# A fixed order for the first half units of a two-layer decoder kernel, filler products in its pause, and a rearranged last tile

## Chip, cores and metric

The kernel runs on one core of a Trainium2 chip. The metric is the device time of one execution in microseconds, as the median of several runs.

## What is computed

The reference is a decoder trunk of two layers on 256 tokens of width 2048, in float32. Layer 0 mixes with RetNet retention (8 heads), layer 1 with MoBA attention (16 heads, one block of 256, so plain causal attention with a bias); each is followed by a gated MLP with a causal convolution of width 3. In short:

```python
for i in range(2):
    hn = rms_norm(h, mix_norm[i])
    h = h + (retention_mixer if i == 0 else moba_mixer)(hn, ...)
    h = h + conv_ffn(rms_norm(h, ffn_norm[i]), ...)
return rms_norm(h, final_norm)        # rms_norm: x * rsqrt(mean(x*x) + 1e-6) * gain
```

The retention mixer begins with `h @ ret_w_in`, whose first columns are q and k of head 0; q and k are rotated by a table of cosines and sines (rope). All weights are float32, about 0.48 GB in all, and each is read once.

## The kernel before, in words

**Products in three parts.** A float32 product is made from rounded high parts and the rest: every operand is split into hi and lo, and hi·hi, hi·lo and lo·hi are summed. ScalarE (ACT) makes the high part `wh` by a copy that rounds (L214); VectorE (DVE) makes the low part `wl = raw - wh` (L215). Both are done by `split_to`.

**Units and half units.** Weights come in units of 1 MB (`raw`, four buffers), issued on SyncE's (SP's) queue in `issue_dma` and `first_dmas`. Each unit is used in halves of 128 x 1024 (a few in four parts). `halves` is the list of all of them in order; `run` (L244) walks through it: for half i it first emits the splits up to i + ahead (`issue_split`), then the products of half i, then what `after` has put off to this point. `ahead` is 0 for i = 0, 2 up to i = 7, and 3 from there. `wh` and `wl` have four buffers each.

**The first eight halves** are q and k of head 0, taken in turn (`emit_pairs`): halves 0, 2, 4, 6 belong to q, halves 1, 3, 5, 7 to k; unit 0 gives halves 0 and 2, unit 1 halves 1 and 3, unit 2 halves 4 and 6, unit 3 halves 5 and 7. Each half has four blocks c, and a block four products (`panel_b`): two with `wh` against 512 columns of `hT` (hi and lo of x beside each other, L329) and two with `wl` against 256 (L332). From half 8 on come the v and g products of head 0 (`panel_s`, L374), which use a scheme with seven products in place of eight for some blocks and need extra sums on DVE.

**hT.** x is transposed by TensorE (PE) in `to_T` (L500, `x_T` calls it) with an identity matrix; ACT multiplies the result by the gain into the high part (L503), DVE makes the low part (L506). The first two chunks of 128 come at the very start (`x_T(0, 2)`), the next two in the middle of half 0 (`rest`, hung into `midway[0]`), four each in the middle of halves 1, 3 and 5.

**The scale.** ACT squares x and sums (`square_t`, L517, `square(j)` for four column blocks j, two instructions each). `make_rB` sums these (L532), adds eps (L525), raises to -1/2 on POOL (L526), and spreads the result over columns: for each of two row tiles DVE makes a diagonal matrix (L541, one buffer for both) and PE multiplies it with ones (L542). `use_rope` multiplies the rope table by it (L685), and `ret_qk` (L700 to L706) turns finished q or k with the table. `ret_begin` puts the squares off to steps 1, 2, 4, 6 and `make_rB` to step 6.

**Order on an engine.** The instructions are traced in the program's order, and a scheduler then lays them out for each engine: earlier traced ones come first among those that it takes to be ready. So a square or a low part may move far ahead of its place in the program, if its inputs are there. Nothing in this kernel fixes an order beyond the data.

**Warm-up.** PE multiplies ones by ones eight times at the start (L630; each float32 product of this kind is two instructions).

**The end.** The last panel gives its results bank by bank; `last_bank` (L894) adds the residual (L904), squares on ACT (L906, the last 512 columns in two pieces of 256), multiplies by the final gain (L911), and after the last piece sums the squares (L914), raises to -1/2 on POOL (L916), scales four column blocks j on ACT (L922, j = 1, and j = 2 for t = 0) or DVE (L924), and stores each (L925) from ACT's queue where ACT scaled, otherwise from SP's.

Of the kernel before, what the change touches and what calls it, by code (L numbers as in the profile page):

```python
# [17 lines left out]
P = 128  # L18
D = 2048
S = 256  # L20
# [6 lines left out]
LOOKAHEAD = 3  # L27
WARMUP = 8


def constants():
# [17 lines left out]
    return {  # L49
        "c_ident": np.eye(P, dtype=np.float32),  # L50
        "c_rope": np.ascontiguousarray(rope),
# [5 lines left out]
def layouts(a):  # L57

    def cols(v):
        return v.reshape(-1, P).T  # L60

    gains = np.concatenate([cols(a["mix_norm"]), cols(a["ffn_norm"]), cols(a["ret_gn"])], 1)
    taps = np.concatenate([a["ffn_conv_w"], a["ffn_conv_b"][:, None]], 1).reshape(2, 4, 2 * NFB, P)
    return {"l_gains": np.ascontiguousarray(gains), "l_taps": np.ascontiguousarray(taps.transpose(3, 0, 1, 2))}
# [31 lines left out]
def build(tc, a, out):  # L96
# [15 lines left out]

    ident = cst.tile([P, P], F32, name="ident")
    h = cst.tile([P, 2, D], F32, name="h")
# [3 lines left out]
    cst.tile([P, 16], F32, name="gap1")  # L118
    gains = cst.tile([P, 96], F32, name="gains")
    cw = [cst.tile([P, 4, 2 * NFB], F32, name=f"cw{i}") for i in range(2)]  # L120
# [62 lines left out]
    def issue_split(i):  # L183
# [8 lines left out]
        if i == 0:  # L192
# [11 lines left out]

            x_T(0, 2)
            split(slice(0, 512))
            midway[0] = rest
        else:
# [4 lines left out]
    def split_to(hi, lo, src):  # L213
        act.activation(hi, src, AF.Copy)  # L214
        dve.tensor_tensor(lo, src, hi.bitcast(F32), op=ALU.subtract)  # L215

# [24 lines left out]
    def after(n, fn):  # L241
        later.append([state["mm"] + n, fn])

    def run():  # L244
        n = len(halves)
        while state["mm"] < n:
            i = state["mm"]
            ahead = 0 if i == 0 else 2 if i < 8 else LOOKAHEAD
            while state["split"] <= min(i + ahead, n - 1):
                issue_split(state["split"])  # L250
                state["split"] += 1
            halves[i]()
            state["mm"] += 1
            while True:
                due = [t for t in later if t[0] <= state["mm"]]
                if not due:
                    break
                later.remove(due[0])
                due[0][1]()
        for t in sorted(later, key=lambda t: t[0]):  # L260
            t[1]()
# [52 lines left out]
    def panel_b(w, n0, xT, done, before=None):  # L314

        box, items = {}, []
        for k0 in range(0, KC, 4):
            def mm(wh, wl, k0=k0):
# [5 lines left out]
                for c in range(4):  # L324
                    k = k0 + c
                    if c == 2 and state["mm"] in midway:
                        midway[state["mm"]]()
                    for b in range(2):
# [160 lines left out]
    def mm3(dst, lh, ll, rh, rl, start, stop):  # L489
        pe.matmul(dst, lhsT=lh, rhs=rh, start=start, stop=False)  # L490
        pe.matmul(dst, lhsT=lh, rhs=rl, start=False, stop=False)  # L491
        pe.matmul(dst, lhsT=ll, rhs=rh, start=False, stop=stop)  # L492

    def to_T(dstT, k0, src, g0, n):

        for c0 in range(0, n, 2):
            pt = aux_tile().rearrange("p (i s) -> p i s", s=S)
            for i in range(2):
                for t in range(2):
                    pe.transpose(pt[:, i, t * P : (t + 1) * P], src(t, c0 + i), ident)  # L500
            for i in range(2):
                g = gains[:, g0 + c0 + i : g0 + c0 + i + 1]
                act.activation(dstT[:, k0 + c0 + i, :S], pt[:, i, :], AF.Copy, scale=g)  # L503
            for i in range(2):
                g = gains[:, g0 + c0 + i : g0 + c0 + i + 1]
                dve.scalar_tensor_tensor(dstT[:, k0 + c0 + i, S:], pt[:, i, :], g,  # L506
                                         dstT[:, k0 + c0 + i, :S].bitcast(F32), op0=ALU.mult, op1=ALU.subtract)
# [4 lines left out]
    def x_T(c0, n):  # L512
        to_T(hT, c0, lambda t, c: h[:, t, (c0 + c) * P : (c0 + c + 1) * P], c0, n)

    def square_t(j, t):
        junk = scr.tile([P, 512], BF16, name="junk")
        act.activation(junk, h[:, t, j * 512 : (j + 1) * 512], AF.Square, accum_out=ssq[:, t, j : j + 1])  # L517

# [100 lines left out]
    dma0 = nc.scalar.dma_start  # L619
    dma0(ident, a["c_ident"])  # L620
    dma0(gains, a["l_gains"])
    dve.memset(ones, 1.0)
# [5 lines left out]
    warmup = aux_tile()  # L628
    for _ in range(WARMUP):
        pe.matmul(warmup[:, :P], lhsT=ones, rhs=ones, start=True, stop=True)  # L630

# [168 lines left out]
    def ret_begin():  # L800
        for i in (1, 2, 3):
            midway[2 * i - 1] = lambda i=i: x_T(4 * i, 4)
        for j in range(4):
            after(1 + j if j < 2 else 2 * j, lambda j=j: square(j))
        after(6, lambda: make_rB(use_rope))
# [88 lines left out]
    def last_bank(t, n, acc):  # L894
# [22 lines left out]
        for j in range(4):  # L917
# [197 lines left out]
```

## Time and profile before

| | us |
|---|---|
| median of 3 runs (2568.09 to 2571.22) | 2570.52 |
| the profiled execution, its own time | 2570.77 |
| its span, first to last instruction | 2569.0 |
| PE busy in the span | 2555.9 (99%) |
| DVE busy | 2072.8 (81%) |
| ACT busy | 1432.1 (56%) |
| mean share of the granted TensorE clock | 0.998 |

Engine names are PE, PEld (weight load, beside PE), DVE, ACT, POOL, SP. A busy share is a mean over stages; the start, the long middle and the end have different limits, and the change touches the first and the last. "Idle before" in a row is the time in which the engine stood still ahead of a group, with the instruction that ended it. Instructions of one kind that follow each other are merged in a timeline; a few matmul records can be missing.

### The profile page before, as it was taken

Reading aid. Unit: us, or ns where it says so; the run is one execution under the profiler, and the core shown is the slowest. Engines: PE = TensorE matmul, PEld = TensorE weight load, DVE = VectorE, ACT = ScalarE, POOL = GpSimd, SP = SyncE. Lnnn points to the kernel's source line nnn. Section 1 sums busy time; section 2 is a strip of 40 time slices with the busy share of each in tenths; the row PEclk is TensorE's granted clock in tenths of the full one; section 3 lists DMA queues with packets and bytes.
Section 4 is the critical chain, followed back from the end, with each engine's and each line's share of the span. In section 5 each row is a group of like instructions: output and inputs, shape, how many; then the busy total and the mean of one; then the engine's idle time right before and its main releaser. Section 6 shows DMA issues by size and latency. Waiting matters only on the chain.

```text
span 2569.0 us, 34327 instructions
## 1 busy us (share of the span) xinstructions
PE 2555.9 (99%) x13288; PEld 2179.2 (85%) x13288; DVE 2072.8 (81%) x2708; ACT 1432.1 (56%) x1848; POOL 10.2 (0%) x24
## 2 busy tenths in 40 slices
PE   9999999999999999999999999999999999999998
PEld 7888888888888888888888888888888888888887
DVE  7888888898877777777988866668877777779897
ACT  6555555555555555555555555455655555555554
POOL 0000000000000000000000000000000000000000
PEclk9999999999999999999999999999999999999999
DMA  7665655555555555555565655555655555556664
GB/s 257 219 200 191 197 184 186 188 181 196 197 197 189 189 190 187 192 186 191 177 215 195 218 192 177 175 182 171 193 194 186 192 187 190 189 188 197 209 200 148
DMA packets 338627, 493.92 MB, mean 192 GB/s; under 512 B 9104, under 2 KB 260000, under 8 KB 338208
## 3 DMA queue, kind: packets, MB, share of 16 engines
q1 hardware_dynamic: 332576, 483.26, 56.9%
q10 hardware_dynamic: 5888, 8.47, 1.1%
q8 instruction: 104, 1.70, 0.3%
q14 instruction: 59, 0.48, 0.1%
HBM read 489.57 MB, written 5.27 MB: 193 GB/s over the span
## 4 chain that ended last, share of the span: by engine, by line
PE 98%; DVE 1%; issue 0%; ACT 0%; DMA 0%; SPq 0%; POOLq 0%; POOL 0%; DVEq 0%; ACTq 0%
PE acc L329 35%; PE aux L374 32%; PE acc L332 17%; PE acc L374 7%; PE acc L295 1%; PE acc L297 1%; PE acc L296 1%; PE aux L500 1%; PE aux L491 0%; PE aux L492 0%; PE aux L490 0%; DVE wl L215 0%; PE acc L500 0%; PE aux L1037 0%; PE acc L491 0%
## 5 line engine op out<-in xcount | busy, mean ns | idle before, releaser
L214 ACT ACTIVATE wh<-raw 128x1024 fp32r<-128x1024 f32 (+1 forms) x1053 | 1073.3, 1030 | 1020.2 <-PE acc L329 454.6
L215 DVE TENSOR_TENSOR wl<-raw,wh 128x1024 fp32r<-128x1024 f32 (+1 forms) x1053 | 1232.2, 1186 | 437.6 <-ACT wh L214 430.5
L329 PE MATMUL acc<-hT,wh 128*128 128x512 f32 x3840 | 1210.6, 397 | 1.4 <-DVE hT L506 1.4
L332 PEld LDWEIGHTS acc<-hT,wl 128*128 128x128 f32 x3840 | 722.7, 188 | 169.9
L332 PE MATMUL acc<-hT,wl 128*128 128x256 f32 x3840 | 756.1, 278 | 0.0
L329 PEld LDWEIGHTS acc<-hT,wh 128*128 128x128 f32 x3840 | 587.6, 189 | 3.5 <-DVE hT L506 1.6
L374 PE MATMUL aux<-wh,actT 128*128 128x512 f32 x1024 | 332.3, 390 | 0.0
L374 PE MATMUL aux<-wh,hT 128*128 128x512 f32 x842 | 280.5, 390 | 0.7 <-ACT wh L214 0.5
L374 PEld LDWEIGHTS aux<-wh,actT 128*128 128x128 f32 x1024 | 192.2, 188 | 40.0 <-DVE h L568 0.3
L374 PE MATMUL aux<-wl,actT 128*128 128x512 f32 x512 | 199.8, 390 | 0.0
L374 PEld LDWEIGHTS aux<-wh,hT 128*128 128x128 f32 x842 | 158.0, 188 | 35.0 <-ACT wh L214 1.9
L374 PE MATMUL aux<-wl,hT 128*128 128x512 f32 x421 | 164.1, 390 | 0.0
L874 DVE SCALAR_TENSOR_TENSOR t<-u,cw,t 128x256 f32<-128x256 f32 x352 | 146.7, 479 | 0.0
L374 PE MATMUL aux<-wh,yT 128*128 128x512 f32 x426 | 141.9, 391 | 0.5 <-ACT yT L214 0.5
L374 PE MATMUL acc<-wh,hT 128*128 128x512 f32 x328 | 120.5, 391 | 0.0
L374 PEld LDWEIGHTS aux<-wl,actT 128*128 128x128 f32 x512 | 96.1, 188 | 20.9 <-DVE wl L215 1.3
L870 ACT ACTIVATE t<-u,cw 128x256 f32<-128x256 f32 x176 | 95.0, 587 | 0.3
L374 PEld LDWEIGHTS aux<-wh,yT 128*128 128x128 f32 x426 | 80.0, 188 | 17.6 <-ACT yT L214 0.8
L374 PEld LDWEIGHTS aux<-wl,hT 128*128 128x128 f32 x421 | 79.1, 188 | 16.5 <-DVE wl L215 0.3
L230 DVE TENSOR_TENSOR raw<-raw 128x1024 f32<-128x1024 f32 x70 | 85.3, 1219 | 0.1
L374 PE MATMUL aux<-wl,yT 128*128 128x512 f32 x213 | 83.0, 390 | 0.0
L690 DVE TENSOR_TENSOR bs<-acc,bs 128x512 f32<-128x512 f32 x120 | 82.0, 683 | 0.0
(202 smaller groups left out, 1985.0 us busy)
## 6 DMA issues: line engine op xcount, KB each, us to landing
raw<-in_ffn_w_up_dram SPq DMA_DIRECT2D x176, 1024.0 KB, 5.2
raw<-in_ffn_w_down_dram SPq DMA_DIRECT2D x88, 1024.0 KB, 5.5
raw<-in_ret_w_in_dram SPq DMA_DIRECT2D x133, 512.0 KB, 4.8
raw<-in_moba_w_qkv_dram SPq DMA_DIRECT2D x48, 1024.0 KB, 5.3
raw<-in_ret_w_out_dram SPq DMA_DIRECT2D x32, 1024.0 KB, 5.5
raw<-in_ret_w_in_dram SPq DMA_DIRECT2D x29, 1024.0 KB, 5.4
raw<-in_moba_w_out_dram SPq DMA_DIRECT2D x16, 1024.0 KB, 5.3
skewD<-tblD ACTq DMA_DIRECT2D x1, 3072.0 KB, 13.2
```

Source lines behind the costliest of these rows:

```text
L214: act.activation(hi, src, AF.Copy)
L215: dve.tensor_tensor(lo, src, hi.bitcast(F32), op=ALU.subtract)
L230: dve.tensor_tensor(b[:, 0:2, :], b[:, 0:4:3, :], b[:, 1:2, :].to_broadcast([P, 2, 512]), op=ALU.add)
L295: pe.matmul(acc, lhsT=xh, rhs=wh[:, c, :], start=(k == 0), stop=False)
L296: pe.matmul(acc, lhsT=xh, rhs=wl[:, c, :], start=False, stop=False)
L297: pe.matmul(acc, lhsT=xl, rhs=wh[:, c, :], start=False, stop=(k == nk - 1))
L329: pe.matmul(acc[:, b, :], lhsT=wh[:, c, b * P : (b + 1) * P], rhs=xt[:, k, :], start=(k == 0), stop=False)
L332: pe.matmul(acc[:, b, S:], lhsT=wl[:, c, b * P : (b + 1) * P], rhs=xt[:, k, :S], start=False, stop=(k == KC - 1))
L374: pe.matmul(acc[b], lhsT=xs, rhs=ws, start=(n == 1), stop=(n == uses[b]))
L690: dve.tensor_tensor(bs, acc[:, :, :S], bs, op=ALU.add)
L870: act.activation(t[:, i, :], u[:, i, 2:], AF.Identity, bias=c[:, 3, b : b + 1], scale=c[:, 2, b : b + 1])
L874: dve.scalar_tensor_tensor(t[:, i, :], u[:, i, tap : tap + S], c[:, tap, b : b + 1], t[:, i, :], op0=ALU.mult, op1=ALU.add)
```

## The change

- The identity matrix and the scale vectors (`gains`) are one tile `laid` and come in one transfer on ACT's queue.
- The first step of `run` (split and products of half 0) lies in a region in which PE, ACT and DVE issue in the traced order. Half 0's first work is traced in smaller pieces: transposes of two chunks, hi(0), `wh` of 256 columns, lo(0), hi(1), `wl` of 256 columns, lo(1), the split of the next 256 columns, then five products of ones by ones (`FILLERS`), then the products. The next two chunks and the rest of the split (`rest`) come at block 1 instead of block 2.
- Until half 8, splits, squares and the transposes of `to_T` are pinned: `in_turn` calls `keep_in_program_order`, which lets an instruction be issued only behind everything traced before it on its engine.
- `ahead` is 1 for i from 1 to 5 (2 before), 2 for i = 6 and 7.
- The squares of x are put off to steps 3, 4, 5, 6 (1, 2, 4, 6 before).
- In `last_bank` the square of the last 256 columns of the last tile is made by DVE (`scalar_tensor_tensor` with a summed result).
- Stores of j = 1 and 2 go out from ACT's queue for both t; before, j = 2 of t = 1 went from SP's.

```diff
-WARMUP = 8
+WARMUP, FILLERS = 8, 5
...
-    gains = np.concatenate([cols(a["mix_norm"]), cols(a["ffn_norm"]), cols(a["ret_gn"])], 1)
+    gains = np.concatenate([np.eye(P, dtype=np.float32), cols(a["mix_norm"]), cols(a["ffn_norm"]), cols(a["ret_gn"])], 1)
...
-    ident = cst.tile([P, P], F32, name="ident")
+    laid = cst.tile([P, P + 96], F32, name="laid")
+    ident, gains = laid[:, :P], laid[:, P:]
...
-            x_T(0, 2)
-            split(slice(0, 512))
-            midway[0] = rest
+            hi, lo = x_T_parts(0, 2)
+            hi(0)
+            act.activation(wh[:, :S], r[:, :S], AF.Copy)
+            lo(0)
+            hi(1)
+            dve.tensor_tensor(wl[:, :S], r[:, :S], wh[:, :S].bitcast(F32), op=ALU.subtract)
+            lo(1)
+            split(slice(S, 512))
+            fillers(FILLERS)
+            midway[0, 1] = rest
...
     def split_to(hi, lo, src):
-        act.activation(hi, src, AF.Copy)
-        dve.tensor_tensor(lo, src, hi.bitcast(F32), op=ALU.subtract)
+        in_turn(act.activation(hi, src, AF.Copy))
+        in_turn(dve.tensor_tensor(lo, src, hi.bitcast(F32), op=ALU.subtract))
...
+    def step(n):
+        i = state["mm"]
+        ahead = 0 if i == 0 else 1 if i < 6 else 2 if i < 8 else LOOKAHEAD
+        while state["split"] <= min(i + ahead, n - 1):
+            issue_split(state["split"])
+            state["split"] += 1
+        halves[i]()
+        state["mm"] += 1
+
     def run():
         n = len(halves)
...
+        with tc.manual_schedule(engines={mybir.EngineType.PE, mybir.EngineType.Activation, mybir.EngineType.DVE}):
+            step(n)
+        while True:
             while True:
                 due = [t for t in later if t[0] <= state["mm"]]
...
+            if state["mm"] == n:
+                break
+            step(n)
...
+    def in_turn(ins):
+
+        if state["mm"] < 8:
+            tc.keep_in_program_order(ins)
+
+    def to_T_parts(dstT, k0, src, g0, n):
...
+            for t in range(2):
+                in_turn(pe.transpose(pts[c][:, t * P : (t + 1) * P], src(t, c), ident))
...
-        act.activation(junk, h[:, t, j * 512 : (j + 1) * 512], AF.Square, accum_out=ssq[:, t, j : j + 1])
+        in_turn(act.activation(junk, h[:, t, j * 512 : (j + 1) * 512], AF.Square, accum_out=ssq[:, t, j : j + 1]))
...
-    dma0(ident, a["c_ident"])
-    dma0(gains, a["l_gains"])
+    dma0(laid, a["l_gains"])
...
+    def fillers(n):
+        for _ in range(n):
+            pe.matmul(warmup[:, :P], lhsT=ones, rhs=ones, start=True, stop=True)
+
+    fillers(WARMUP)
...
-            midway[2 * i - 1] = lambda i=i: x_T(4 * i, 4)
+            midway[2 * i - 1, 2] = lambda i=i: x_T(4 * i, 4)
         for j in range(4):
-            after(1 + j if j < 2 else 2 * j, lambda j=j: square(j))
+            after(3 + j, lambda j=j: square(j))
         after(6, lambda: make_rB(use_rope))
...
             junk = scr.tile([P, 512], BF16, name="junk")
+            if n and t and i:
+                dve.scalar_tensor_tensor(junk[:, sl], hs[:, sl], 1.0, hs[:, sl], op0=ALU.mult, op1=ALU.mult,
+                                         accum_out=sq[:, 4:5])
+                continue
             act.activation(junk[:, sl], hs[:, sl], AF.Square, accum_out=sq[:, 2 + n + i : 3 + n + i])
...
-            (dma0 if by_act else nc.sync.dma_start)(o[:, t, sl], h[:, t, sl])
+            (dma0 if j in (1, 2) else nc.sync.dma_start)(o[:, t, sl], h[:, t, sl])
```

## Rows read from the trace of the kernel before

**Rows 1.** The chain of work that ended last, by engine, from the profile's page.

```profile
PE 98%; DVE 1%; issue 0%; ACT 0%; DMA 0%; SPq 0%; POOLq 0%; POOL 0%; DVEq 0%; ACTq 0%
```

**Rows 2.** Busy time of each engine in two stretches. After the stretch and its length: busy us (instructions) of PE, PEld, DVE, ACT, POOL, then the granted clock, the DMA share and GB/s.

```profile
35.09:62.70 27.61, 27.13 (x129) 22.39 (x128) 27.34 (x43) 13.20 (x17) 0.00 (x0) 1.00 0.50 166
65.00:2554.00 2489.00, 2488.88 (x12957) 2123.12 (x12958) 2014.91 (x2611) 1387.17 (x1768) 8.09 (x16) 1.00 0.58 191
```

**Rows 3.** The timeline of PE at the start: start, length, engine, line, operation, count, and the idle time before it.

```profile
1.05 3.50 PE L630 MATMUL aux<-ones 128*128 128x128 f32 x16 [1.05 <-DVE ones L622]
...
6.21 0.66 PE L500 MATMUL aux<-ident,h 128*128 128x128 f32 x4 [1.23 <-DMA h<-in_x_dram]
8.28 1.22 PE L329 MATMUL acc<-hT,wh 128*128 128x512 f32 x2 [1.41 <-DVE hT L506]
```

**Rows 4.** Busy time by stretch, columns as in rows 2; here the third number from the end (the granted clock) matters.

```profile
7.00:8.00 1.00, 0.00 (x0) 0.00 (x0) 0.26 (x1) 1.00 (x4) 0.00 (x0) 0.76 1.06 378
8.00:9.00 1.00, 0.72 (x2) 0.63 (x3) 1.00 (x4) 0.95 (x3) 0.00 (x0) 0.50 1.01 312
...
14.00:15.00 1.00, 1.00 (x6) 0.89 (x6) 0.64 (x1) 0.00 (x0) 0.00 (x0) 0.82 1.10 359
```

**Rows 5.** The chain of waits in order of time, first 40 us: start, time that the piece takes on the chain, what it is and how many instructions.

```profile
9.93 0.85 PE acc L329 x2
10.78 0.43 PE acc L332 x2
...
15.50 0.87 PE aux L500 x8
16.37 0.47 PE acc L329 x2
...
27.25 0.47 PE acc L329 x2
...
32.79 0.22 PE aux L542 x2
...
36.98 2.75 PE aux L374 x12
```

**Rows 6.** What PE waited for in the whole span: who waited for whom, us in total, times, the longest. The other rows of this view are the pauses of rows 3 and the wait before the warm-up.

```profile
PE aux L374 <- ACT wh L214: 0.5, 2, 0.3
PE aux L374 <- ACT yT L214: 0.5, 1, 0.5
```

**Rows 7.** The timelines of ACT and DVE between 6 and 12 us, columns as in rows 3.

```profile
6.26 0.63 ACT L517 ACTIVATE junk<-h 128x512 bf16<-128x512 f32 x1 [0.25 <-DMA h<-in_x_dram]
...
6.89 1.55 ACT L503 ACTIVATE hT<-aux,gains 128x256 fp32r<-128x256 f32 x4
...
9.26 1.06 ACT L214 ACTIVATE wh<-raw 128x1024 fp32r<-128x1024 f32 x1 [0.30 <-DMA raw<-in_ret_w_in_dram]
...
10.35 1.23 DVE L215 TENSOR_TENSOR wl<-raw,wh 128x1024 fp32r<-128x1024 f32 x1 [0.35 <-ACT wh L214]
```

**Rows 8.** Transfers issued in the first 60 us: queue, count, KB of each, median us from issue to landing; and SP's own timeline row of the one transfer of 1024 KB (unit 3).

```profile
raw<-in_ret_w_in_dram SPq DMA_DIRECT2D x1, 1024.0 KB, 11.5
...
ident<-in_c_ident_dram ACTq DMA_DIRECT2D x1, 64.0 KB, 3.2
gains<-in_l_gains_dram ACTq DMA_DIRECT2D x1, 48.0 KB, 4.0
...
10.86 1.41 SPq L164 DMA_DIRECT2D raw<-in_ret_w_in_dram  x1
```

**Rows 9.** The end of the last square of x on ACT (the read of its sum) and the first diagonal on DVE, from the timelines.

```profile
21.99 0.18 ACT L517 ACTIVATION_READ_ACCUMULATOR junk<-h 128x1 f32 x1
...
23.45 0.29 DVE L541 TENSOR_SCALAR diag<-ident,r 128x128 f32<-128x128 f32 x1 [0.89 <-POOL r L526]
```

**Rows 10.** DVE's timeline from 25 to 36 us, and PE's row of the second product with a diagonal.

```profile
25.23 3.48 DVE L215 TENSOR_TENSOR wl<-raw,wh 128x1024 fp32r<-128x1024 f32 x3
...
32.63 0.38 PE L542 MATMUL aux<-diag,ones 128*128 128x128 f32 x2
...
33.05 0.69 DVE L685 TENSOR_TENSOR rope<-rope,aux 128x512 f32<-128x512 f32 x1 [0.41 <-PE aux L542]
...
35.09 1.23 DVE L215 TENSOR_TENSOR wl<-raw,wh 128x1024 fp32r<-128x1024 f32 x1 [0.22 <-ACT wh L214]
```

**Rows 11.** The end: timeline rows of DVE, ACT and SP, and the busy time of the slice from 2567 to 2568 us, columns as in rows 2.

```profile
2560.79 0.75 DVE L904 TENSOR_TENSOR h<-aux,h 128x256 f32<-128x256 f32 x2 [0.23 <-PE aux L374]
...
2561.58 0.69 DVE L911 TENSOR_TENSOR hg<-h,fn 128x512 f32<-128x512 f32 x1
...
2562.17 0.19 ACT L906 ACTIVATION_READ_ACCUMULATOR junk<-h 128x1 f32 x1
...
2562.39 0.16 DVE L914 TENSOR_REDUCE vf<-sq 128x1 f32<-128x5 f32 x1
...
2563.92 1.40 SPq L925 DMA_DIRECT2D out_dram<-h  x3
...
2567.00:2568.00 1.00, 0.00 (x0) 0.00 (x0) 0.00 (x0) 0.00 (x0) 0.00 (x0) 0.50 0.51 195
```

**Rows 12.** The costliest groups of the page, one row: line, engine, operation, shapes, count, busy us, mean ns of one, idle before.

```profile
L874 DVE SCALAR_TENSOR_TENSOR t<-u,cw,t 128x256 f32<-128x256 f32 x352 | 146.7, 479 | 0.0
```

More of the change, by code (lines that the diff above doesn't have):

```diff
@@ L49, in constants @@
     return {
-        "c_ident": np.eye(P, dtype=np.float32),
         "c_rope": np.ascontiguousarray(rope),
@@ L118, in build @@
     cst.tile([P, 16], F32, name="gap1")
-    gains = cst.tile([P, 96], F32, name="gains")
     cw = [cst.tile([P, 4, 2 * NFB], F32, name=f"cw{i}") for i in range(2)]
@@ L242, in after @@
         later.append([state["mm"] + n, fn])
+    def step(n):
[6 more added lines that the diff above has]
+        state["mm"] += 1
     def run():
         n = len(halves)
[L246 to L253, printed above, removed]
+        with tc.manual_schedule(engines={mybir.EngineType.PE, mybir.EngineType.Activation, mybir.EngineType.DVE}):
+            step(n)
+        while True:
             while True:
@@ L325, in mm @@
                     k = k0 + c
-                    if c == 2 and state["mm"] in midway:
-                        midway[state["mm"]]()
+                    if (state["mm"], c) in midway:
+                        midway[state["mm"], c]()
                     for b in range(2):
@@ L492, in mm3, with hi, lo @@
         pe.matmul(dst, lhsT=ll, rhs=rh, start=False, stop=stop)
+    def in_turn(ins):
+        if state["mm"] < 8:
+            tc.keep_in_program_order(ins)
+    def to_T_parts(dstT, k0, src, g0, n):
+        pts = []
+        for c in range(n):
+            if c % 2 == 0:
+                pt = aux_tile().rearrange("p (i s) -> p i s", s=S)
+            pts.append(pt[:, c % 2, :])
+            for t in range(2):
+                in_turn(pe.transpose(pts[c][:, t * P : (t + 1) * P], src(t, c), ident))
+        def hi(i):
+            act.activation(dstT[:, k0 + i, :S], pts[i], AF.Copy, scale=gains[:, g0 + i : g0 + i + 1])
+        def lo(i):
+            dve.scalar_tensor_tensor(dstT[:, k0 + i, S:], pts[i], gains[:, g0 + i : g0 + i + 1],
+                                     dstT[:, k0 + i, :S].bitcast(F32), op0=ALU.mult, op1=ALU.subtract)
+        return hi, lo
@@ L494, in to_T @@
     def to_T(dstT, k0, src, g0, n):
         for c0 in range(0, n, 2):
[L497 to L507, printed above, removed]
+            hi, lo = to_T_parts(dstT, k0 + c0, lambda t, c: src(t, c0 + c), g0 + c0, 2)
@@ L509, in h_T, with x_T, x_T_parts @@
+            for part in (hi, lo):
+                for i in range(2):
+                    part(i)
     def h_T(j, g0):
         to_T(hT, 4 * j, lambda t, c: h[:, t, (4 * j + c) * P : (4 * j + c + 1) * P], g0 + 4 * j, 4)
-    def x_T(c0, n):
-        to_T(hT, c0, lambda t, c: h[:, t, (c0 + c) * P : (c0 + c + 1) * P], c0, n)
+    def x_T(c0, n, how=to_T):
+        return how(hT, c0, lambda t, c: h[:, t, (c0 + c) * P : (c0 + c + 1) * P], c0, n)
+    def x_T_parts(c0, n):
+        return x_T(c0, n, to_T_parts)
@@ L628, in build @@
     warmup = aux_tile()
-    for _ in range(WARMUP):
-        pe.matmul(warmup[:, :P], lhsT=ones, rhs=ones, start=True, stop=True)
+    def fillers(n):
+        for _ in range(n):
+            pe.matmul(warmup[:, :P], lhsT=ones, rhs=ones, start=True, stop=True)
+    fillers(WARMUP)
     dram = ctx.enter_context(tc.tile_pool(name="dram", bufs=1, space=bass.MemoryType.DRAM))
```

## The prediction

> **What bounds the kernel now.** I read the chain of waits first: TensorE (PE) carries 98% of the span [rows 1]. Then busy time by stretch: from 65 to 2554 us PE is busy 2488.88 of 2489.00 us [rows 2]. The reader should see that nothing in that stretch can be won without taking products away, and the change takes none away. What is left are the two ends.
>
> At the start PE does its warm-up products and four transposes, and then stands 1.23 us for a piece of x and 1.41 us for hT; its first real product is at 8.28 us [rows 3]. The record of the granted clock shows the price: 0.76 over the slice from 7 to 8 us, so half (1.2 GHz) from about 7.5; 0.50 in the slice from 8 to 9; and 0.82 from 14 to 15, so full (2.4 GHz) again at about 14.4 [rows 4]. A block of four products (two of 512 columns, two of 256) takes 0.85 + 0.43 = 1.28 us at half; at full the two wide ones take 0.47 [rows 5], and with the narrow ones in proportion it is 0.70. So the pauses and the half clock are what the first half units lose.
>
> Between 35 and 63 us another engine sets the pace: VectorE (DVE) is busy 27.34 of 27.61 us [rows 2], and PE waits there and just after, 0.5 us for an hT-like operand (yT) and 0.5 us for wh, about 1.0 us together [rows 6]. This matters most below: time won by PE before 35 us is kept only if DVE comes early too.
>
> At the end PE stops near 2560.8 us; after it comes a chain of DVE and ScalarE (ACT) steps, the power on POOL, the scaling and the stores [rows 11].
>
> **The start, step by step.** Today ACT squares x ahead of the first hT (6.26 to 6.89 us) [rows 7]. The new order puts hT and the first 256-column splits first, so I put the first product near 6.2 us: transposes by about 5.0, an ACT copy and a DVE subtraction of about 0.5 us each after them, twice over. The two constants come in one transfer of 112 KB; the parts landed 3.2 and 4.0 us after issue [rows 8], and the transposes stand behind the warm-up anyway, so I cost it at nothing. The five fillers are ten instructions. Two of that shape take 0.22 us at full clock [rows 5], so 1.1 us, inside the pause of 1.23 us; at the pace of the warm-up (16 in 3.50 us [rows 3]) 2.2 us, which would put the first product about 1 us later, still ahead of today. I take full clock, since the pause is what they fill and the clock fell only after it.
>
> The lead does not reach the full 5 us. Half 1 needs raw data that lands just before 9.26 us, where ACT starts on it; ACT takes 1.06 and DVE 1.23 us, and the low part was there at 11.58 [rows 7]. Landing is set by transfers that fill the DMA engines (share 1.06 and 1.01 [rows 4]), and the change leaves SP's order of them alone; ACT's queue only loses one issue. The transposes of the next two chunks (0.66 us [rows 3]) now come behind block 0, in time that PE has before that data. So the low products of half 1 start at 11.5 at best, their first two blocks end at 11.5 + 0.23 + 0.70 = 12.45 us, and today the transposes behind those blocks start at 15.50 [rows 5]: a lead of 3.0 us. Half 5 begins today at 27.25 [rows 5], then at 24.2; its data was issued at 10.86 and landed 11.5 us later, 22.4 [rows 8], and ACT and DVE have it split by about 24.8. The lead holds until there.
>
> **Where I expect it to be given back.** Splits below half 8 are now pinned behind everything traced before them on their engine. With the lookahead of one, half 7 is split in step 6, after the fourth square and make_rB, which are traced at the end of step 5. So on DVE the low parts of halves 7 and 8 must stand behind the whole scale chain: sum, power on POOL, diagonal, PE product, second diagonal (same buffer), PE product, and the multiply of rope. Today the scheduler is free: the squares are done at 22.2 and the scale is there at 23.4, and the low parts of 5, 6, 7 run at 25.23, long before rope at 33.05 [rows 9, 10].
>
> Worked out: half 5 ends two blocks at 24.85 + 0.23 + 0.70 = 25.8; eight transposes 0.87 us; the four hT copies on ACT 1.57 us, starting after the first four transposes, end at 27.85; the fourth pair of squares, pinned behind them, takes 1.5 us (two of 0.63 and their reads of 0.18, one overlapped with the other [rows 7, 9]) and ends at 29.3. From there to the first diagonal it took 1.28 us (22.17 to 23.45): 30.6. From the first diagonal's start to rope's end: 0.29 us, a PE product and its hand-over 0.42 (32.63 to 33.05), again 0.29 and 0.42, then 0.69: 32.7 [rows 9, 10]. The low part of half 7 then ends at about 33.9. PE has finished half 6 at 30.9 and half 7's first two products at 31.4, and waits some 2.5 us. Half 7 ends near 36.3 instead of 36.98 [rows 5]: PE keeps 0.7 us of its 3.0.
>
> DVE does worse. At 33.9 it still owes the low parts of 8 and 9, 1.15 us each (pace of three in 3.48); today both are done when it starts the next one at 35.09 [rows 10]. It gets there at 36.2: 1.1 us late, then runs the 27 us in which it has no slack. Its idle 0.27 us there may shrink, and half 9, pinned behind q's last subtraction, may add the 0.6 us of an ACT copy; I take neither. PE's lead can't help, since PE waits for DVE in that stretch already. **Start: +1.1 us.** The bounds are the two readings of the pin: −3.0 (no wait behind it, whole lead kept) and +2.7 (the clock falls all the same, below).
>
> What is hidden: ACT's splits 7 and 8 wait behind the squares, but DVE's part is later; the moved squares (eight of about 0.7 us) lie in ACT's free time; SP's queue is not pinned.
>
> **The end.** Today the two half squares of the last tile run on ACT one after the other, and DVE's product hg (0.69) runs beside them; the sum starts at 2562.39, when the second read ends [rows 11]. With the second square on DVE, the order as traced is add, square, hg, sum. The adds end at 2561.5; a like operation of 256 columns took 0.479 [rows 12], paced at 0.42; hg 0.60 to 0.69: the sum at 2562.55 to 2562.7. What ACT no longer does, DVE now does in front of hg. If the scheduler puts the sum first, it starts at about 2562.0. Range −0.4 to +0.4, taken +0.2 (order as traced). No row shows what an accumulated result costs on DVE: on ACT its read took 0.19 us, which is the upper end; the lower is nothing. The Trainium skill (VectorE: DVE Perf Modes, section on two Vector instructions with no wait between them) makes such an operation two instructions; by that the end would be about +0.4 rather than +0.2, which is inside the range.
>
> One store of the last four moves from SP's queue to ACT's. SP issues three in 1.40 us, the last by 2565.3, but bytes still flow at 195 GB/s on average through the slice 2567 to 2568 [rows 11]. So the transfers set the end, and I cost the move at nothing. The Trainium skill (DMA: Bandwidth & Descriptors, Issuing engines are not separate DMA queues) says several issuing engines save the issue time only; that would be at most one issue, −0.4 us, and the rows show even this hidden.
>
> **Sum.** +1.1 + 0.2 = +1.3 us. The profiled execution took 2570.77 us (span 2569.0 and 1.77 around it), so 2572.1 for it; the median of the runs, 2570.52, is 0.25 lower, so **2571.8 us**. A measurement of this kernel can tell about 0.2%, 5.1 us, from no change.
>
> **Rivals.**
> 1. The pin does not bite, because the fourth square and the scale chain come early enough. For: free to move, squares and scale were done at 22.2 and 23.4 [rows 9], long before rope was needed; and DVE stood idle for several of the waits named in these rows, so it could follow PE. Against: the trace order of step 5 and step 6. Then −3.0 + 0.2: 2567.7 us.
> 2. The clock falls in the first pause in spite of the fillers. For: transposes stood between the two pauses and didn't hold it [rows 3, 4]; PE still waits about 0.8 and 0.5 us for the second half of unit 0 and 0.5 to 1 us for half 1. Then the end of half 1 comes only 1.4 us early instead of 3.0, and all behind it 1.6 us later: 2573.4 us.
> 3. Slower: PE's new wait of 2.5 us before half 7 is as long as today's two pauses together, and drops the clock a second time. It was at half for 6.9 us (7.5 to 14.4); spent on products all through, that costs 3.4. PE then stands at −0.7 + 3.4 = +2.7 some halves later, takes back at most the 1.0 us it waits today, and ends at +1.7 to +2.7; with rival 2 (1.6) as well +3.3 to +4.3. That decides once PE's lateness is over DVE's 1.1 us. With the end's +0.2 that is 2572.2 to 2575.0, taken 2573.5; slower by over 5.1 us only if the clock stays low some 2 us longer than at the start today.
> 4. The pins change no order that matters and the fillers run at half clock: about 2570.5 us.
>
> **How the numbers follow.** Forecast 0.45, rival 1 0.27, rival 2 0.13, rival 3 0.10, rival 4 0.05. The forecast's own range is 2570.3 to 2573.3. The runs shown spread by 3 us, so the range takes in rival 1 less 0.7 and rival 3: 2567.0 to 2575.0. None of the cases wins 5.1 us: faster 0.03; slower 0.06 from rival 3's tail; within 0.2% 0.91.
>
> **What would show it.** Right: clock at full between 7.5 and 14.4; first product near 6.2; half 5 near 24.2; then PE idle for over 2 us just before half 7's low products, with DVE idle around the diagonals, and rope directly ahead of a wl. Wrong: no PE wait between 28 and 37 us, or the products of head 0 (L374) starting before 35 us with DVE keeping up. At the end: the sum of squares later than hg or not. The forecast falls if PE busy from 65 us on is no longer complete.

## The result, and the profile after

| | before | after |
|---|---|---|
| median, us (lowest to highest) | 2569.95 (2568.09 to 2571.22) | 2586.8 (2586.47 to 2587.13) |
| ratio, 95% interval | | 1.0066 [1.0054, 1.0079] |
| the profiled execution, its own time; its span | 2570.77; 2569.0 | 2587.04; 2585.2 |
| PE busy | 2555.9 | 2571.1 |

Both medians are of six runs. The kernel became slower by 16.9 us; 2571.8 had been forecast, with 2575.0 as the upper end. The profiled executions differ by 16.3 us in their own time and 15.2 us in PE's busy time: PE waits about 1 us more in all, and its work takes 15 us longer.

**Where it arises.** The same weight transfer (counted among the weight transfers of SP's queue, from 0) is issued in both traces when the same buffer comes free. Its issue time after minus its issue time before is how late the kernel is there. Growth of that lateness by stage, in us, each stage bounded by a transfer (no. 30, 195, 283, 400, 483 and 523, issued before at 88, 707, 1194, 1860, 2323 and 2537 us), worked out from the traces, for the changed kernel and for the experiments below:

```
                       start  retention  up 0  down 0+MoBA  up 1  down 1
after                   +2.3     +8.1    +0.1     +3.7       0.0   +1.7
e1  two tiles           +2.1      0.0     0.0      0.0       0.0   +0.1
e2  h and hT +384       -0.5     +8.0    +0.1     +3.6       0.0   +1.6
e3  hT +384             -0.7     +8.0    +0.2     +3.8       0.0   +1.6
e8  hT -64              -1.7     +2.8    -2.1     -0.2      -2.2   +0.3
e11 hT +64              -1.1     +7.7    -4.2     +1.8      -4.4   +1.6
e12 hT +448             -1.1     +2.8    -2.2     -0.2      -2.2   +0.4
e13 hT +512             -1.2      0.0     0.0      0.0       0.0    0.0
e14 all +64             -1.4     +0.1     0.0     +0.1       0.0    0.0
e15 better start, +448  -2.2     +2.7    -2.1     -0.2      -2.2   +0.3
e16 after, hT +448      +2.8     +2.8    -2.2     -0.3      -2.2   +0.3
```

So +2.3 us of the 16.3 come from the start, +0.4 from what lies behind the last weight transfer, and 13.6 from the long middle that I had called untouched. The start column is measured against one execution of the kernel before, and a late one: e2, e3, e8 and e11 to e14 have its program at the start, and theirs comes 0.5 to 1.7 us earlier. Against those the changed start is 2.8 to 4.0 us late. In the up panels hT streams against loaded slices of the weights (`panel_b`); in the retention mixer most products load slices of hT (or of other tiles) and stream the weights (`panel_s`); the down panels load actT and, for some blocks, hT.

**The middle.** Busy time by stretch of the changed kernel (columns as in rows 2), and its groups of products (line, operation, tiles, shapes, count; busy us, mean ns of one; idle before):

```profile
65.00:735.00 670.00, 669.55 (x3195) 556.21 (x3195) 588.56 (x748) 364.45 (x432) 5.75 (x9) 1.00 0.58 192
735.00:1195.00 460.00, 460.00 (x2640) 402.25 (x2640) 344.96 (x460) 262.18 (x343) 0.83 (x3) 1.00 0.58 187
```

```profile
L343 PE MATMUL acc<-hT,wh 128*128 128x512 f32 x3840 | 1198.8, 393 | 1.1 <-DVE hT L528 0.8
L346 PE MATMUL acc<-hT,wl 128*128 128x256 f32 x3840 | 762.3, 280 | 0.5 <-DVE wl L221 0.5
L388 PE MATMUL aux<-wh,actT 128*128 128x512 f32 x1024 | 332.7, 390 | 0.0
L388 PE MATMUL aux<-wh,hT 128*128 128x512 f32 x842 | 286.3, 397 | 1.5 <-ACT wh L220 1.5
L388 PE MATMUL aux<-wl,hT 128*128 128x512 f32 x421 | 166.3, 395 | 0.3 <-DVE wl L221 0.3
```

The same groups of the kernel before, which the prediction did not read by operand:

```profile
L329 PE MATMUL acc<-hT,wh 128*128 128x512 f32 x3840 | 1210.6, 397 | 1.4 <-DVE hT L506 1.4
L332 PE MATMUL acc<-hT,wl 128*128 128x256 f32 x3840 | 756.1, 278 | 0.0
...
L374 PE MATMUL aux<-wh,actT 128*128 128x512 f32 x1024 | 332.3, 390 | 0.0
L374 PE MATMUL aux<-wh,hT 128*128 128x512 f32 x842 | 280.5, 390 | 0.7 <-ACT wh L214 0.5
...
L374 PE MATMUL aux<-wl,hT 128*128 128x512 f32 x421 | 164.1, 390 | 0.0
```

PE is as good as fully busy and at full clock, as before [rows 2]. But the products of `panel_s` with hT went from 390 to 397 and 395 ns, while those with actT, from the same line and of the same shape, stayed at 390. (These durations overlap. From the start of one product to the start of the next, in the mean over the middle, products with a loaded slice of hT went from 229.0 to 234.8 ns where `wh` streams and from 227.2 to 232.2 where `wl` does. These two sums grow by 10.9 us of the 13.6; products that stream hT take 7.3 us less in sum against `wh` and 7.9 us more against `wl`.) One thing distinguishes hT from actT here: `laid` holds 896 bytes per partition where `ident` held 512, and the `gains` that it took in lay behind hT. So hT moved by 384 bytes, and actT and the weight tiles did not move.

**The start.** PE's timeline after (columns as in rows 3) with its waits, the clock by stretch, then work of DVE and of ACT between 31 and 43 us:

```profile
5.36 1.28 PE L665 MATMUL aux<-ones 128*128 128x128 f32 x10
6.69 0.71 PE L343 MATMUL acc<-hT,wh 128*128 128x512 f32 x2
...
31.60 0.46 PE L576 MATMUL aux<-diag,ones 128*128 128x128 f32 x2 [0.88 <-DVE diag L575]
...
34.84 0.51 PE L346 MATMUL acc<-hT,wl 128*128 128x256 f32 x2 [0.30 <-DVE wl L221]
...
40.31 1.20 PE L388 MATMUL aux<-wh,hT 128*128 128x512 f32 x4 [1.00 <-ACT wh L220]
41.83 0.50 PE L388 MATMUL aux<-wl,hT 128*128 128x512 f32 x1 [0.32 <-DVE wl L221]
```

```profile
7.00:8.00 1.00, 1.00 (x9) 0.94 (x8) 0.82 (x2) 0.36 (x2) 0.00 (x0) 1.00 1.04 363
8.00:9.00 1.00, 0.78 (x5) 0.49 (x4) 0.01 (x1) 0.88 (x3) 0.00 (x0) 1.00 1.02 353
```

```profile
31.17 0.29 DVE L575 TENSOR_SCALAR diag<-laid,r 128x128 f32<-128x128 f32 x1 [0.89 <-POOL r L560]
32.10 0.29 DVE L575 TENSOR_SCALAR diag<-laid,r 128x128 f32<-128x128 f32 x1 [0.65 <-PE aux L576]
32.97 0.69 DVE L722 TENSOR_TENSOR rope<-rope,aux 128x512 f32<-128x512 f32 x1 [0.58 <-PE aux L576]
33.57 2.35 DVE L221 TENSOR_TENSOR wl<-raw,wh 128x1024 fp32r<-128x1024 f32 x2
...
39.34 0.69 DVE L743 TENSOR_TENSOR qT<-m,qT 128x512 fp32r<-128x512 f32 x1
...
40.56 1.22 DVE L221 TENSOR_TENSOR wl<-raw,wh 128x1024 fp32r<-128x1024 f32 x1
```

```profile
38.68 0.63 ACT L742 ACTIVATE qT<-m 128x512 fp32r<-128x512 f32 x1
39.22 3.89 ACT L220 ACTIVATE wh<-raw 128x1024 fp32r<-128x1024 f32 x4
```

The clock stays at full (2.4 GHz) where it was at half before [rows 4]. The first product comes 1.6 us earlier than before [rows 3]. Then the chain of diagonals and rope stands directly ahead of the low parts of halves 7 and 8, as forecast. Half 9 stands behind q on both engines: its high part behind q's copy at 38.68 on ACT, its low part behind q's last subtraction at 39.34 on DVE. PE's longest wait, 1.00 us at 40.31, is for that high part.

**The end.** DVE after (columns as in rows 3):

```profile
2576.78 0.76 DVE L941 TENSOR_TENSOR h<-aux,h 128x256 f32<-128x256 f32 x2
2577.56 0.69 DVE L952 TENSOR_TENSOR hg<-h,fn 128x512 f32<-128x512 f32 x1
2578.18 0.42 DVE L944 SCALAR_TENSOR_TENSOR junk<-h 128x256 bf16<-128x256 f32 x1
2578.52 0.08 DVE L944 DVE_READ_ACCUMULATOR junk<-h 128x1 f32 x1
2578.63 0.16 DVE L955 TENSOR_REDUCE vf<-sq 128x1 f32<-128x5 f32 x1
```

From the add to the sum it is 1.85 us, against 1.60 before [rows 11].

### The profile page after: what moved, and what is told of

The parts are those of the page before. It is cut to its first block, busy times and chain, and to the rows that moved or that the text cites. A ratio compares the mean times of both kernels' runs of the same rounds, so it can differ in the third digit from the quotient of the medians.

```text
span 2585.2 us, 34340 instructions
## 1 busy us (share of the span) xinstructions
PE 2571.1 (99%) x13298; PEld 2183.5 (84%) x13298; DVE 2075.4 (80%) x2711; ACT 1433.3 (55%) x1847; POOL 10.2 (0%) x24
## 4 chain that ended last, share of the span: by engine, by line
PE 98%; DVE 1%; issue 0%; ACT 0%; DMA 0%; SPq 0%; POOL 0%; POOLq 0%; DVEq 0%; ACTq 0%
PE acc L343 34%; PE aux L388 32%; PE acc L346 17%; PE acc L388 7%; PE acc L311 1%; PE acc L309 1%; PE acc L310 1%; PE aux L522 1%; DVE wl L221 0%; PE aux L505 0%; PE aux L506 0%; PE aux L504 0%; PE acc L522 0%; PE aux L1078 0%; PE aux L665 0%
## 5 line engine op out<-in xcount | busy, mean ns | idle before, releaser
L220 ACT ACTIVATE wh<-raw 128x1024 fp32r<-128x1024 f32 (+2 forms) x1053 | 1074.3, 1030 | 1030.4 <-PE acc L343 449.2
L221 DVE TENSOR_TENSOR wl<-raw,wh 128x1024 fp32r<-128x1024 f32 (+2 forms) x1053 | 1231.8, 1185 | 444.8 <-ACT wh L220 443.4
L388 PE MATMUL aux<-wh,hT 128*128 128x512 f32 x842 | 286.3, 397 | 1.5 <-ACT wh L220 1.5
```

The lines of the kernel that those rows point to most:

```text
L220: in_turn(act.activation(hi, src, AF.Copy))
L221: in_turn(dve.tensor_tensor(lo, src, hi.bitcast(F32), op=ALU.subtract))
L388: pe.matmul(acc[b], lhsT=xs, rhs=ws, start=(n == 1), stop=(n == uses[b]))
```

## The experiments: the middle

**e1: two tiles again**, in the changed kernel, at their old places and with two transfers; all else of the change stays.

```diff
-    laid = cst.tile([P, P + 96], F32, name="laid")
-    ident, gains = laid[:, :P], laid[:, P:]
+    ident = cst.tile([P, P], F32, name="ident")
...
     cst.tile([P, 16], F32, name="gap1")
+    gains = cst.tile([P, 96], F32, name="gains")
...
-    dma0(laid, a["l_gains"])
+    dma0(ident, a["l_gains"][:, :P])
+    dma0(gains, a["l_gains"][:, P:])
```

> The changed kernel with identity and scale vectors again in two tiles and two transfers, at the places that they had before; all else as changed. Theory (address): joining them moved h and hT by 384 bytes, and products that hold a slice of hT as stationary operand while wh or wl streams became about 7 ns slower each; putting the tiles back gives back the growth between 88 and 2520 us, some 13.5 us: about 2573 us, with the start still some 2 us later than before. Rival (order): the pins upset the scheduler's order through the whole kernel; then the time stays near 2587 us. Rival (transfer): the joined transfer delays something at the start only; then about 2586 us.

Measured: 2573.32 us (2573.14 to 2573.95), ratio 1.0015 [1.0006, 1.0024]. The lateness stays at 2.1 to 2.2 us from 88 us to the last weight transfer, and the group of products is back at 390 ns:

```profile
L388 PE MATMUL aux<-wh,hT 128*128 128x512 f32 x842 | 281.0, 390 | 1.7 <-ACT wh L220 1.6
```

**e2: the kernel before with `gains` right behind `ident`; e3: the same with `gains` between gap0 and hT**, so that hT moves by 384 bytes and h does not. No instruction of the program differs in either. The edit of e3:

```diff
     cst.tile([P, 16], F32, name="gap0")
+    gains = cst.tile([P, 96], F32, name="gains")
     hT = cst.tile([P, KC, 2 * S], F32R, name="hT")
     cst.tile([P, 16], F32, name="gap1")
-    gains = cst.tile([P, 96], F32, name="gains")
```

> The kernel before with one line moved: the tile of the scale vectors is allocated right behind the identity, so that h and hT lie 384 bytes higher, as in the changed kernel; two transfers, no other edit. Theory (address): about 2570 + 13.5 = 2583 us, growing in the stages whose stationary operand lies in hT and flat in the up projections. Rival (order) and rival (transfer): 2570 us.

> The kernel before with the tile of the scale vectors allocated between gap0 and hT: hT lies 384 bytes higher, h and everything behind stay. Theory (address of hT): as e2, about 2583 us. Rival (address of h): h is read by transposes and residual adds only; then 2570 us here and 2583 in e2.

Measured: 2583.45 us, ratio 1.0054 [1.0039, 1.0069], and 2584.14 us, 1.0059 [1.0043, 1.0076]. e3 alone brings the whole loss of the middle (8.0 + 0.2 + 3.8 + 1.6 = 13.6 us): it is hT's place, not h's, not the transfer, not the order.

**e8, e11, e12, e13: hT moved by other amounts** in the kernel before, with all behind it in place: −64 bytes (gap0 out, gap1 doubled), +64 (the reverse), +448 (`gains` and both gaps in front), +512 (`ones` in front). The edit of e11; the others are made in the same way:

```diff
-    cst.tile([P, 16], F32, name="gap0")
+    cst.tile([P, 32], F32, name="gap0")
     hT = cst.tile([P, KC, 2 * S], F32R, name="hT")
-    cst.tile([P, 16], F32, name="gap1")
```

> The kernel before with gap0 taken out and gap1 twice as long: hT lies 64 bytes lower, all else stays. If only the shift by 384 bytes is unlucky, 2570 us as before; if any move of hT from its place costs, 2575 us or more. No figure is to be had from the rows; taken as 2 to 1 for a cost, since a gap of 64 bytes was put there.

> The kernel before with the gap ahead of hT 64 bytes larger and the gap behind it gone, so that hT alone moves up by 64 bytes. Theory 1, the cost grows with the distance moved: 384 bytes cost 14 us, so 64 bytes cost about 2.3 us: 2572.3. Theory 2, a place within a block of some size decides, and 64 bytes are enough to leave a good one: about 14 us more, 2584. Theory 3, small moves trade the two kinds of stages against each other, as 64 bytes down did: within 2 us of the kernel before, with products of a slice of hT against weights and those that stream hT moving in opposite directions.

> The kernel before with hT moved up by 448 bytes (384 for the scale vectors ahead of it, and 64 of gap), everything behind it in its old place. Theory 1, the cost grows with the distance: 16 us, 2586. Theory 2, the place within 512 bytes decides: 448 up is 64 down, which gave 2568.2; so 2567 to 2570. Theory 3, anything beyond a small move costs the same 14 us: 2584.

> The kernel before with the 512-byte tile ones moved from behind hT to ahead of it, so that hT moves up by 512 bytes and the weight tiles stay. If the place modulo 512 bytes decides: 2569.3, as the kernel before, and no drift between the two traces over the retention mixer or either up panel (within 0.5 us). If 448 up was good by chance and the distance counts: between 2568 and 2590, with a drift in the stages that use hT.

Measured: 2568.15 us (0.9995 [0.9986, 1.0005]); 2572.25 (1.0011 [1.0002, 1.0021]); 2568.19 (0.9995 [0.9986, 1.0004]); 2569.68 (1.0003 [0.9993, 1.0012]). For e8 I had held a cost to be likelier, 2 to 1; the middle came out 1.4 us shorter. e11's median is the one that theory 1 gave, 2572.3, and would have misled. The table above tells more than the medians: from the retention mixer on, +448 and −64 agree stage by stage to 0.1 us, and +512 is the kernel before to 0.1 us. So these moves act by their place within 512 bytes, not by their distance. And a place has no one price: 64 bytes up costs the retention mixer 7.7 us and gives 4.2 and 4.4 us back in the up panels. By group, e11's products with loaded slices of hT are as slow as those after, and those in which hT streams take 1955.0 us (the first two rows), against 1966.7 before:

```profile
L328 PE MATMUL acc<-hT,wh 128*128 128x512 f32 x3840 | 1196.0, 393 | 1.4 <-DVE hT L505 1.4
L331 PE MATMUL acc<-hT,wl 128*128 128x256 f32 x3840 | 759.0, 279 | 0.0
...
L373 PE MATMUL aux<-wh,hT 128*128 128x512 f32 x842 | 285.8, 396 | 0.3 <-ACT wh L213 0.2
```

**e14: hT and everything behind it, the weight tiles too, 64 bytes up together** (gap0 doubled, gap1 kept).

> The kernel before with the gap ahead of hT 64 bytes larger and the gap behind it kept, so that hT and every tile behind it, the weight tiles among them, move up by 64 bytes together. If hT's place relative to the weight tiles decides: 2569.3 and no drift. If its own place decides: as with hT alone moved by 64, that is +7.9 us over the retention mixer, -4.1 over the up panel of layer 0, -3.7 over that of layer 1, and 2572 in all.

Measured: 2569.57 us, ratio 0.9999 [0.9990, 1.0008], no stage drifts by over 0.2 us, and the group is at 390 ns:

```profile
L374 PE MATMUL aux<-wh,hT 128*128 128x512 f32 x842 | 280.4, 390 | 0.7 <-ACT wh L214 0.6
```

It is hT's place relative to tiles behind it that counts. Which of them (`wh` and `wl`, which PE reads with hT, or `raw`, which the transfers fill) was not separated by a run. The traces narrow it. Between 100 and 700 us, the median from a product with a loaded slice of hT and `wh` streaming to the next is 227 ns before and 232 ns after. It is the same two numbers for the products during which no DMA packet moves (152 in either trace) as for the rest, and with ACT idle as with ACT busy. So a collision with transfers or with ACT does not explain the 5 ns, and PE's own reading of hT together with `wh` or `wl` is the likelier pair; that stays an argument.

**e16: the changed kernel with gap1's 64 bytes in front of hT**, so +448 in place of +384; nothing else.

> The changed kernel with its merged tile, and only the 64 bytes of gap behind hT moved to the front of it, so that hT lies 448 bytes up instead of 384 and all else stays. If the place relative to the weight tiles, modulo 512 bytes, is the whole cause: 2586.8 - 13.5 - 1.1 = 2572.2 us. If the merged tile or its transfer has a share in the 13.5: above 2573.

Measured: 2571.82 us (2571.22 to 2572.25), ratio 1.0011 [1.0001, 1.0020]. A gap of 64 bytes takes 15 us off the changed kernel with its merged tile kept. The tile and its one transfer cost nothing that this shows; where they push hT does.

## The experiments: the start and the end

All of these stand on e1, so that the middle is as before.

**e4: half 7 split a step earlier; e6: that, and the squares at steps 1 to 4 in place of 3 to 6** (pins kept). **e5: no pins. e7: no fillers.**

The edits, in this order: e4 and e6 (first pair), e6 (second), e5 (third), e7 (last).

```diff
-        ahead = 0 if i == 0 else 1 if i < 6 else 2 if i < 8 else LOOKAHEAD
+        ahead = 0 if i == 0 else 1 if i < 5 else 2 if i < 8 else LOOKAHEAD
...
-            after(3 + j, lambda j=j: square(j))
+            after(1 + j, lambda j=j: square(j))
...
-        if state["mm"] < 8:
-            tc.keep_in_program_order(ins)
+        pass
...
-WARMUP, FILLERS = 8, 5
+WARMUP, FILLERS = 8, 0
```

> As e1 (two tiles), and the lookahead is 2 from step 5 on, so that half 7 is split, and traced, ahead of the fourth square and the scale chain. Theory (pin): PE no longer waits for half 7's low part behind rope, DVE fills its wait for the scale with it, and unit 6's transfer is issued earlier; the start gives back the 2 us and more: 2 to 4 us below e1, near 2570. Rival (the start is late for another reason, such as landing times): within 0.5 us of e1.

> As e4 (two tiles, half 7 split in step 5), and the four pairs of squares come at steps 1 to 4 in place of 3 to 6, pins kept. Theory (the late fourth square holds the scale chain, and the chain holds DVE): rope's multiply comes some 3 us earlier relative to half 7, and of the 1.3 us that e4's start is still late all goes and some lead is kept: 1 to 3 us below e4, 2569.5 to 2571.5. Rival (what is left in e4 is the pin of half 9 behind q): equal to e4 within 0.5 us.

> As e1 (two tiles), and no instruction outside the first step is pinned: the scheduler is free again for splits, squares and transposes; the region of the first step, the fillers and the lookahead stay as changed. Theory (pins delay squares, rope and the low parts of halves 7 to 9, and DVE has no slack behind): the squares go forward and nearly the whole lead of 3 us is kept: e1 less 4 to 5 us, about 2568 to 2569 us. Rival (the lookahead of one, or the region, makes the start late): within 1 us of e1, 2573 us.

> As e1 (two tiles) without the five fillers. Theory (fillers hold the clock): the granted clock falls to half within the first 10 us, and half 5 begins 1 to 2 us later than in e1; the end is then late by the same 1 to 2 us, as DVE has no slack behind it: 2574 to 2575 us. Rival (the shorter pauses alone hold it): clock at full, same time as e1 within 0.5 us.

Measured: e4 2572.37 us (1.0011 [1.0001, 1.0020]); e6 2571.29 (1.0009 [0.9999, 1.0018]); e5 2568.97 (0.9998 [0.9988, 1.0007]); e7 2573.37 (1.0016 [1.0007, 1.0026]). Against e1's 2573.32 the early split gives 1.0 us, the early squares 1.1 more, and no pins 4.35. The groups of experiments ran at different times, and the median of the kernel before beside them lay between 2568.7 and 2569.6; but the lateness at 88 us, from the traces, goes the same way: +2.1 in e1, +1.3 in e4, +0.1 in e6, −2.1 in e5, +1.9 in e7. In DVE's rows rope comes at 33.31 in e4, 31.57 in e6, 31.00 in e5 (32.97 after). e4 gave back less than its theory wanted: half 7's low part was out of the chain's way, but half 9 was still behind q on ACT and DVE, and so it was in e6. Without pins DVE does more before 35.09 us. Busy time from 5.6 to 35.09 (columns as in rows 2), e1, then e5:

```profile
5.60:35.09 29.49, 26.73 (x158) 22.23 (x158) 18.51 (x32) 21.21 (x44) 0.70 (x1) 1.00 0.95 334
```

```profile
5.60:35.09 29.49, 27.36 (x167) 23.80 (x166) 21.68 (x36) 23.06 (x47) 0.70 (x1) 1.00 1.06 376
```

DVE has done 3.17 us less in e1. From there to 62.70 it is busy for 27.39 of 27.61 us in e1 (27.51 in e5), so it cannot take that back, and PE waits for it. This accounts for most of the 4.35 us; the rest was not assigned.

**e7** fell out against my theory that the fillers hold the clock: the pause with no fillers in it was 1.42 us, ahead of the product at 6.55, and the granted clock stayed at 1.00 up to 15 us in its profile. **e10** asks the same without pins, beside **e9** (e5 with the last tile as before, the second square on ACT).

```diff
-            if n and t and i:
-                dve.scalar_tensor_tensor(junk[:, sl], hs[:, sl], 1.0, hs[:, sl], op0=ALU.mult, op1=ALU.mult,
-                                         accum_out=sq[:, 4:5])
-                continue
...
-            (dma0 if j in (1, 2) else nc.sync.dma_start)(o[:, t, sl], h[:, t, sl])
+            (dma0 if by_act else nc.sync.dma_start)(o[:, t, sl], h[:, t, sl])
```

> The version with two tiles and without pins, and besides with the last tile as before (second square on ScalarE, the store of j = 2, t = 1 from SP's queue). Theory: the end of the changed kernel costs 0.25 us (from the add to the sum of squares 1.85 us against 1.60), so 2568.7 us against 2569.0 with the new tail, and the stretch from the add to the sum is 1.60 us again. Rival: the tail only moves the scheduler's choice elsewhere, and the span from the last add to the end stays at 8.4 us.

> As the run before it, with no filler products in the first pause. In the run with pins and no fillers the granted clock stayed at full although the pause was 1.42 us. Theory 1: the clock stays at full here too, and the time is within 0.5 us of the version with fillers, or up to 1 us less where the fillers stood ahead of a product. Theory 2: the fillers are what keeps the clock up when nothing is pinned; then the slices from 7 to 10 us show 0.50 and the time is 1.5 to 3.4 us more.

Measured: e9 2568.69 us (2568.41 to 2569.00; 0.9997 [0.9988, 1.0007]), e10 2569.59 (2569.33 to 2570.53; 1.0001 [0.9992, 1.0011]). e10's pause was 2.26 us, and the clock fell behind it, at about 9.4 us, to come back at about 12.8 us. That is theory 2, though its half clock was to come earlier and to cost 1.5 to 3.4 us; it cost 0.9. The first product is late in all three, at 7.94 in e10, 7.87 in e9 and 7.96 in e5, the latter two with the fillers in the pause. The timeline of PE in e10, then in e5:

```profile
7.94 0.70 PE L343 MATMUL acc<-hT,wh 128*128 128x512 f32 x2 [2.26 <-DVE hT L527]
```

```profile
4.92 1.28 PE L665 MATMUL aux<-ones 128*128 128x128 f32 x10
7.96 0.70 PE L343 MATMUL acc<-hT,wh 128*128 128x512 f32 x2 [1.76 <-DVE hT L527]
```

and the stretches behind the first product, of e10, then of e5 (the granted clock is the third number from the end):

```profile
9.00:10.00 1.00, 1.00 (x5) 0.77 (x4) 0.41 (x2) 0.65 (x2) 0.00 (x0) 0.69 1.04 349
10.00:11.00 1.00, 1.00 (x5) 0.75 (x4) 0.77 (x2) 1.00 (x3) 0.00 (x0) 0.50 1.08 375
```

```profile
9.00:10.00 1.00, 1.00 (x8) 0.79 (x6) 0.42 (x2) 0.63 (x2) 0.00 (x0) 1.00 1.04 345
```

The fillers are worth 0.9 us where hT is free to come late. Where the fixed order brings it early, e7's median is e1's to 0.05 us; but three of e7's ten runs took 2574.4 to 2574.6, above all of e1's, and no trace shows why. The old tail gives 0.28 us of median, and as much from the last weight transfer to the end of the trace, and the trace of e9 shows it at its place, 1.60 us from add to sum as before:

```profile
2558.69 0.76 DVE L941 TENSOR_TENSOR h<-aux,h 128x256 f32<-128x256 f32 x2 [0.23 <-PE aux L388]
...
2560.29 0.16 DVE L951 TENSOR_REDUCE vf<-sq 128x1 f32<-128x5 f32 x1
```

**e15: e9 with hT 448 bytes up**, the better start and the better place together.

> The version with two tiles, no pins, the fillers and the old tail, with hT 448 bytes higher. The two gains lie in different stages, so they add: 2568.7 - 1.1 = 2567.6 us. Rival: the products of hT in the first half units are among those that this place makes slower, and the result is 2568.7 or more.

Measured: 2567.27 us (2567.10 to 2567.40), ratio 0.9993 [0.9983, 1.0002]. The two gains add: 2568.69 − 1.4, and in the table a start 2.2 us and a middle 1.5 us shorter. All its runs are below 2567.94, the lowest of the kernel before beside it, and its median is 2.3 us below that kernel's; the interval of the ratio still takes in 1.

## Why the prediction was wrong

**The step that failed** is in the part on the start: "the two constants come in one transfer …, so I cost it at nothing", and, with it, the statement that nothing can happen from 65 to 2554 us because no product is added or removed. I priced the merged tile as a transfer and never asked where the tiles behind it land. Its price was 13.6 us, 83% of the loss: e3 shows it alone, e1 and e16 take it out. No rival had it. The test named at the close, PE busy no longer complete, did not see it either: PE stayed complete and each product took longer. The views that show it are mean ns of one by operand and the drift of the same transfer between two traces.

**The start** was right in kind and half the size: +2.3 for +1.1, against the same profiled execution (2.8 to 4.0 against the earlier starts in the table).
- Right: full clock from the start on; the first product at 6.69 (forecast 6.2); half 5's wait for its low part at 25.27 (24.85); the first diagonal at 31.17 (30.6), rope's end near 33.66 (32.7); the low parts of 7 and 8 right behind it. PE's waits there are smaller than the 2.5 us forecast (0.88 and 0.30), because PE took high-part products of half 7 and of head 0 out of turn in between.
- Mis-sized: half 9 behind q, named and then left out ("I take neither"). With its cover gone PE waits 1.00 us for the high part and 0.32 for the low part, at 40.31 and 41.83. The pins together cost 4.35 us (e5 against e1): 1.0 by the split of half 7, 1.1 by the squares, 2.3 by the rest.
- Rivals: 1 did not come, since the pins bite; e5, which takes them out, shows what it would have given, 2568.97 against 2567.7 worked out. 2 and 3 did not come either: the clock does not fall at all, neither in the first pause nor before half 7. (Rival 3's lower end should read 2572.4: 2570.52 + 1.7 + 0.2.)

**The end** was right in size and in its reason, that DVE now does the square as well as hg ahead of the sum: +0.25 for +0.2. The order was as traced, except that hg came before the square. The sum took in an accumulator read on DVE of 0.08 us, against 0.19 on ACT [rows 11]. The Trainium skill (VectorE: DVE Perf Modes, Two Vector instructions with no wait between them) says that such an operation is two instructions, and the trace agrees. The +0.4 that I put beside it, with ACT's 0.19 us for the second one, was too much.

## What to carry to other kernels

A tile that is merged, grown or dropped moves every tile allocated behind it, and that can cost more than the work that the merge saves: list the bytes that each operand of the long stage moves by, relative to the tiles it is read with, and keep them with a gap where nothing else is known. When PE is fully busy in both traces, compare the mean time of one product by operand before anything else. And an order that pins an engine's work must be read to the end: here the pins held splits behind a chain that was free to come early.

## What was not expected of the hardware

- hT's place relative to the tiles behind it changes the pace of products with a loaded slice of hT by 2 to 3% (for +384, 229.0 to 234.8 and 227.2 to 232.2 ns from start to start). The places behave as if they repeated every 512 bytes: +448 equals −64, and +512 equals 0. Sums over the middle: +384 13.6 us, +64 2.5, −64 and +448 −1.4. The Trainium skill (SBUF — State Buffer, SBUF: two separate sides) says that PE never waits on anyone at its ports. It speaks there of contention between engines, and of no cost of an operand's place; e3 and e11 show such a cost. The Trainium skill (SBUF — State Buffer, Specifications (TRN2)) gives lines of 16 bytes; all these moves are multiples of 64 bytes, so they leave hT's place within such a line as it was. The mechanism is open.
- The start of the kernel before is not steady. With the same program at the start, the clock was at half from about 7.5 to 14.4 us in its profile [rows 4], from about 9 to 12.4 in e13's, and never in e8's; the stretches where e13's clock falls and rises, and e8's from 9 to 10 us:

```profile
8.00:9.00 1.00, 0.74 (x4) 0.65 (x5) 1.00 (x4) 1.00 (x4) 0.00 (x0) 0.97 0.95 297
9.00:10.00 1.00, 1.00 (x4) 0.82 (x4) 1.00 (x3) 1.00 (x2) 0.00 (x0) 0.50 1.02 356
...
12.00:13.00 1.00, 1.00 (x7) 0.92 (x7) 0.01 (x1) 0.95 (x2) 0.00 (x0) 0.82 1.07 380
```

```profile
9.00:10.00 1.00, 1.00 (x8) 0.84 (x7) 0.96 (x2) 0.02 (x1) 0.00 (x0) 1.00 1.00 345
```

Its runs spread by 3.6 us (2567.8 to 2571.4 over 119 runs beside the experiments), those of e9 and e15, whose clock does not fall in their profiles, by 0.6 and 0.3. The clock is a part of the spread and not all of it: the 47 runs with a mean granted clock of 0.998 took 2569.9 us in the mean, the 72 with 0.999 took 2568.9, but these 72 alone go from 2567.8 to 2571.2. In the profiles with this start PE's pause for a piece of x differs too, 0.29 us in e14 and 1.23 before [rows 3].
